# A decoder layer on Trainium2: the output projection's second norm, the order of the change to the up-projection, and the samples by DMA

## Chip, cores, metric

The kernel runs on one core of one Trainium2 chip. The metric is device microseconds of one execution, as the median of several.

## The reference, cut to what matters

One layer of a decoder: 1024 prompt tokens and 32 sample tokens (8 sequences of 4), model width 1024, feed-forward width 2816, all in float32.

```
x = x + gate1 * RMSNorm(Mix(RMSNorm(x) * (1 + scale1) + shift1))
x = x + gate2 * RMSNorm(ConvFFN(RMSNorm(x) * (1 + scale2) + shift2))

Mix:     mix = concat(pool_mixer, gated_conv, silu(layer_norm(conv31))) @ w_out
ConvFFN: up = h @ w_up
         gate, val = split(causal_dwconv3(up, past_ffn))
         ff = (silu(gate) * val) @ w_down
```

What is computed does not change. The change is in the layer norm of the third group of Mix, in the output projection with the norms behind it, and in the up-projection.

## The kernel before, in words

**Numbers.** Each float32 operand is split into two parts, high and low (`*_hi` is a cast on ACT, the scalar engine; `*_lo` is a subtraction on DVE, the vector engine), and a product takes three passes on PE, the tensor engine: high by high, high by low, low by high.

**Order.** Instructions of PE, ACT, DVE and SP (the engine that issues most DMAs) run in the order in which the program emits them. From the output projection on, this order is written by hand: `at(t, f, ...)` notes a step under a planned time `t`, and `play` emits all steps sorted by it. The planned times serve to sort; an engine works through its list and waits where a value is missing.

**Layer norm.** The variance of 1056 tokens goes through POOL as 96 rows of 11 (`ln_rstd`, L438) and comes back as a row by three small DMAs (L444). `ln_bc` (L446) spreads a third of the row over 128 partitions by a PE product with ones, into a PSUM buffer of `psb`, and `ln_apply` (L452) multiplies. After these come the loads of `w_out` row blocks 0, 1, 5, 6, 7 (`w_load`, L785) on SP, the pool mixer's products (`proj`, L605), the silu on ACT, and the products `mm2` (L833) of tiles 0 to 2 with `w_out` row blocks 2, 3, 4, then 1, 0, then 5, 6, 7. There are two buffers of `psb`.

**Output projection.** Eight tiles of 128 tokens and one of 32 (tile 8, the samples); a tile's product is 8 row blocks. `chain` (L962) lays out what follows for a tile: `sq1`, `rs` (sum of squares, then the scale by a power on POOL, L865), `gt`, `res` (L882, first norm and residual), `sq2`, `rs`, `xn2` (L889, product with the second scale), `tr` (L897, eight PE transpositions), `mod` (L911 on ACT or L908 on DVE), `h2_hi`, `h2_lo` (the split). Tiles come in pairs: `t13` and `t24` (L943, L948) form differences of an even and an odd tile, and `t_hi`, `t_lo` split these.

**Up-projection.** For each of 22 column tiles (gate and value, 128 columns each) a seven-product scheme: products 1 to 7 (`prod`, L1209, twelve PE steps each) take sums and differences of weight blocks (`s_sum`, `s_hi`, `s_lo`) and of token tiles. Product 1, 6, 5 and 3 accumulate one after the other in the first bank of one PSUM tile, product 2 takes its second bank, products 7 and 4 take the tile `U["z"]`. `snap` "a", "b", "c" (L1223, ACT) keep the first bank in between, `c11`, `c22`, `c21` (DVE, L1233) and `c12` (ACT, L1239) form the four blocks. The convolution `tap0`, `taps2` (L1280), `silu`, `gated` and `fsum` follow.

**Samples.** `smp` (L1253) multiplies the 32 sample tokens with both weight tiles, into one PSUM tile; `smp_ev` copies that to SBUF on ACT, `smp_t` (L1262) turns and sums it on PE by a product with `sel`, and `smp_out` (L1266) copies the result to the convolution's input.

**At the change of stage.** Products 1 and 2 of column tiles 0 and 1 come first (from planned time `t8`); between the first two stands `tr` of tile 7. Then from `b = t8 + 4 * DP` products 6, 5, 7, 3, 4 of tile 0, with `tr` of tile 8 and the samples of tiles 0 and 1 among them:

```
sample(0, b + DP + 0.9, b + 3 * DP + 2 * DS)
sample(1, b + 2 * DP + DS + 0.9, b + 4 * DP + 2 * DS, b + 5 * DP + 2 * DS + 7.0)
seq = [(prod, 0, 6), (DS + 0.9,), (prod, 0, 5), (DS,), (prod, 0, 7), (prod, 0, 3), (prod, 0, 4)]
```

In the loop of the later tiles the order on PE is product 6, samples of the next tile, 7, 5, product 1 of the next tile, 3, product 2 of the next tile, 4.

Of the kernel before, what the change touches and what calls it, by code (L numbers as in the profile page):

```python
# [10 lines left out]
F32 = mybir.dt.float32  # L11
# [39 lines left out]
def body(ctx: ExitStack, tc: tile.TileContext, a, o):  # L51
# [17 lines left out]
    one1 = lnp.tile([P, P], F32, name="one1")  # L69
# [11 lines left out]
    dve.memset(one1, 1.0)  # L81
# [9 lines left out]
    gd = tc.dram_tile([9, 2048], F32, name="gd")  # L91

# [860 lines left out]
    def t_hi(i):  # L953
        act.copy(ycol(0, i), h2_of(i))

    def t_lo(i):
        sub_to(ycol(1, i), h2_of(i), ycol(0, i).bitcast(F32))
# [4 lines left out]
    def chain(i, e, tt):  # L962
# [6 lines left out]
        at(e + 5.5, xn2, i)  # L969
# [3 lines left out]
        at(tt + 1.1, mod, i, 1)  # L973
        at(tt + 2.5, h2_hi, i)
        if i % 2:
            at(tt + 2.5, t13, i)
            at(tt + 3.0, h2_lo, i)
            at(tt + 3.6, t24, i)
# [3 lines left out]
        else:  # L982
            at(tt + 3.5, h2_lo, i)

    def chain_s(e):
        for dt, f in ((0, sq1), (2.2, rs), (2.4, gt), (3.7, res), (4.9, sq2), (6.0, rs), (6.8, xn2)):
            at(e + dt, f, 8)
        for q in range(2):
            at(e + 11.74, tr, 8, q)
            at(e + 12.4 + 0.1 * q, mod, 8, q)  # L990
# [59 lines left out]
    for k in (2, 3, 4):  # L1050
        for i in range(3):
# [4 lines left out]
            if k == 3:  # L1056
                at(t, ln_bc, i)
# [38 lines left out]
    for n, i in enumerate(order):  # L1096
# [16 lines left out]
    fs = {p: tc.dram_tile([FT // 2, P, 512], F32, name=f"fs{p}") for p in range(1, 8)}  # L1113
    U = {}
# [16 lines left out]
    def open_b():  # L1131
# [77 lines left out]
    def prod(i, p):  # L1209
# [5 lines left out]
        for k in range(4):  # L1215
# [5 lines left out]
    def snap(i, n):  # L1221
        t = pools["p3" if n == "a" else "p3b"].tile([P, 512], F32, name=f"sn{n}", bufs=1)
# [33 lines left out]
    def smp_ev(i):  # L1256
        t = pools["p3"].tile([P, P], F32, name="smp", bufs=2)
        act.copy(t, U["s"][:, P * (i % 2):P * (i % 2) + P])
        U["smp", i] = t

    def smp_t(i):
        pe.matmul(U["s"][:, 256:320], lhsT=U["smp", i], rhs=U["sel"].rearrange("p a n -> p (a n)"), start=True, stop=True)  # L1262

    def smp_out(i, v):
        e = e_of(i, v)
        act.copy(ext_parts(e, 2)[2], U["s"][:, 256 + 32 * v:288 + 32 * v].rearrange("p (s t) -> p s t", t=ST))  # L1266
# [59 lines left out]
    DP, DS = 2.75, 1.6  # L1326
# [7 lines left out]
    at(t8 + 14.5, open_z)  # L1334
    at(t8 + 14.51, open_b)
# [445 lines left out]
```

## Time and profile before

| | us |
|---|---|
| median of 3 runs (lowest, highest) | 1061.47 (1061.19, 1062.1) |
| the profiled execution | 1063.64 |
| its span, first to last instruction | 1061.8 |
| mean granted TensorE clock | 0.992 |
| PE busy | 1030.5 (97%) |
| DVE busy | 825.0 (78%) |
| ACT busy | 466.6 (44%) |
| POOL busy | 38.2 (4%) |
| DMA queue 1, share of 16 engines | 39.0% |

One execution is profiled; stretches and single instructions are read from it, while the median comes from other runs. Busy time of PE overlaps between neighbouring steps, so the distance of two starts tells what a step costs, and waits are listed by the engine that waits and the instruction that ended them. A granted clock of 1.00 is 2.4 GHz, 0.50 is 1.2 GHz.

### The profile page before, as it was taken

What the parts mean: (1) busy time and instruction counts of PE and PEld (TensorE: products, weight loads), DVE (VectorE), ACT (ScalarE), POOL (GpSimd) and SP (SyncE); (2) the same over time, 40 slices, a digit from 0 to 9 for tenths busy, and PEclk for the clock granted to TensorE, in tenths of its full rate; (3) what the DMA queues carried; (4) which work ended last, traced back from release to release, by engine and by line L of the source; (5) the groups of instructions that cost most, each with busy time, mean ns of one, the idle gap of its engine ahead of it and who ended that gap; (6) DMA issues with size and microseconds to landing.
All of it is one profiled execution on the core that took longest, in us unless ns stands there. A gap on an engine that the chain in (4) does not pass through costs nothing. (4 is left out here: it accounts for less than half of the span.)

```text
span 1061.8 us, 15512 instructions
## 1 busy us (share of the span) xinstructions
PE 1030.5 (97%) x6094; PEld 864.8 (81%) x6094; DVE 825.0 (78%) x1142; ACT 466.6 (44%) x835; POOL 38.2 (4%) x56
## 2 busy tenths in 40 slices
PE   5999999999999989999999999999999999999997
PEld 4999989997687668888888888888888787778885
DVE  5688898978547788888788788778878764987584
ACT  6331111115747745445454444544545464335551
POOL 3000000001011100000000000000000000020100
PEclk9999999999999989999999999999999999999999
DMA  8776652211512413323314223322323694325272
GB/s 334 262 228 194 193 185 88 63 41 17 184 43 99 156 54 99 109 64 127 110 60 129 91 79 115 104 80 92 114 74 110 228 412 179 109 73 161 90 267 100
DMA packets 68050, 141.10 MB, mean 133 GB/s; under 512 B 17156, under 2 KB 28676, under 8 KB 64904
## 3 DMA queue, kind: packets, MB, share of 16 engines
q1 hardware_dynamic: 66632, 135.77, 39.0%
q10 hardware_dynamic: 1344, 4.33, 1.0%
q8 instruction: 48, 0.79, 0.3%
q14 instruction: 26, 0.21, 0.1%
HBM read 110.18 MB, written 29.90 MB: 132 GB/s over the span
## 5 line engine op out<-in xcount | busy, mean ns | idle before, releaser
L1280 DVE SCALAR_TENSOR_TENSOR facc<-fext,par,facc 128x1072 f32<-128x1072 f32 x88 | 117.2, 1332 | 14.2 <-ACT facc L1273 12.7
L535 DVE SCALAR_TENSOR_TENSOR yb<-cext,par,yb 128x1024 f32<-128x1024 f32 x90 | 111.9, 1278 | 0.8
L279 PE MATMUL psa<-hh,whi 128*128 128x352 f32 x372 | 82.0, 328 | 0.0
L279 PE MATMUL psa<-hh,wlo 128*128 128x352 f32 x372 | 80.2, 323 | 0.0
L1532 PE MATMUL psd<-whi 128*128 128x512 f32 x204 | 80.1, 393 | 0.0
L279 PE MATMUL psa<-hl,whi 128*128 128x352 f32 x372 | 80.1, 323 | 0.0
L1532 PE MATMUL psd<-whi,wlo 128*128 128x512 f32 x204 | 79.6, 390 | 0.1
L1532 PE MATMUL psd<-wlo,whi 128*128 128x512 f32 x204 | 79.5, 390 | 0.1
L1513 ACT CAST whi<-fa 128x512 fp32r<-128x512 f32 x73 | 45.3, 621 | 70.9 <-PE psb L1532 24.6
L927 DVE TENSOR_TENSOR wlo<-fa,whi 128x512 fp32r<-128x512 f32 x73 | 49.9, 684 | 31.0 <-ACT whi L1513 31.0
L1218 PE MATMUL psc<-hh,sh 128*128 128x512 f32 x176 | 69.7, 396 | 2.8 <-DVE fext L1233 2.8
L1218 PE MATMUL psb<-hh,sh 128*128 128x512 f32 x176 | 71.3, 405 | 0.0
L1218 PE MATMUL psc<-hl,sh 128*128 128x512 f32 x176 | 69.6, 396 | 0.9 <-DVE hl L927 0.9
L1218 PE MATMUL psc<-hh,sl 128*128 128x512 f32 x176 | 69.4, 395 | 0.0
L1218 PE MATMUL psb<-hh,sl 128*128 128x512 f32 x176 | 68.8, 391 | 0.0
L1218 PE MATMUL psc<-bh,whi 128*128 128x512 f32 x176 | 68.6, 390 | 0.0
L1218 PE MATMUL psc<-bh,wlo 128*128 128x512 f32 x176 | 68.5, 389 | 0.0
L1218 PE MATMUL psc<-bl,whi 128*128 128x512 f32 x176 | 68.5, 389 | 0.0
L1218 PE MATMUL psb<-hl,sh 128*128 128x512 f32 x176 | 68.5, 389 | 0.0
L279 PEld LDWEIGHTS psa<-hh,whi 128*128 128x128 f32 x372 | 62.8, 189 | 6.4 <-issue 4.1
L279 PEld LDWEIGHTS psa<-hh,wlo 128*128 128x128 f32 x372 | 63.8, 188 | 0.0
L279 PEld LDWEIGHTS psa<-hl,whi 128*128 128x128 f32 x372 | 63.1, 188 | 0.0
(270 smaller groups left out, 2318.0 us busy)
## 6 DMA issues: line engine op xcount, KB each, us to landing
fa<-fs SPq DMA_DIRECT2D x73, 256.0 KB, 3.8
adaw<-in_ada SPq DMA_DIRECT2D x16, 1024.0 KB, 7.5
raw<-in_w_up SPq DMA_DIRECT2D x22, 512.0 KB, 3.6
rawb<-in_w_up SPq DMA_DIRECT2D x22, 512.0 KB, 3.7
fs<-facc SPq DMA_DIRECT2D x44, 256.0 KB, 2.5
b<-in_w_down SPq DMA_DIRECT2D x18, 512.0 KB, 7.3
fs<-whi SPq DMA_DIRECT2D x33, 256.0 KB, 2.3
adaw<-in_adag SPq DMA_DIRECT2D x8, 1024.0 KB, 7.1
```

The costliest lines, as they stand in the source:

```text
L279: pe.matmul(ps[:, c, 0:CW], lhsT=wt[:, k, :], rhs=h[:, k, c * CW:(c + 1) * CW], start=(k == 0 and n == 0), stop=(k == KT - 1 and n == 2))
L535: dve.scalar_tensor_tensor(out=y[:, 0:NPR], in0=e[:, k:k + NPR], scalar=par[:, off + k:off + k + 1], in1=y[:, 0:NPR], op0=ALU.mult, op1=AL ...
L927: dve.tensor_tensor(out=out, in0=x, in1=y, op=ALU.subtract)
L1218: pe.matmul(out, lhsT=w[:, ks], rhs=h(k), start=(p in (1, 2, 7) and k == 0 and n == 0), stop=(k == 3 and n == 2), skip_group_check=True)
L1280: dve.scalar_tensor_tensor(out=acc[:, 0:1072], in0=e[:, k:k + 1072], scalar=par[:, wo + k:wo + k + 1], in1=acc[:, 0:1072], op0=ALU.mult, o ...
L1513: act.copy(hi[:, 0:512], R[n, "raw"])
L1532: pe.matmul(ps, lhsT=s[:, cs], rhs=w, start=(first and m == 0), stop=(j == HK - 1 and m == 2), skip_group_check=True)
```

## The change

- The layer norm's row goes to DRAM by one DMA and comes back to all 128 partitions by a second, in place of three DMAs and the three products of `ln_bc`.
- `xn2` is sorted ahead of `h2_lo` of the tile before (planned 4.95 instead of 5.5 after the chain's start, `h2_lo` half a microsecond later); `t24` becomes `t2` and `t4`, and `t_hi`, `t_lo` can take half a tile.
- At the change of stage the order on PE becomes products 6, 7, three quarters of 5, `tr` of tile 8 (into the samples' PSUM tile), the rest of 5, both sample groups, 3, 4. Three lists give the order on DVE and ACT around it. Some temporary tiles move to buffers that are free then.
- `smp_ev` becomes a DVE transposition (in blocks of 32 by 32), a DMA to DRAM, and `smp_ld` brings four loads that gather the turned block; `smp_out` adds two pieces on DVE. `smp_t` and `sel` go, in all 22 column tiles.
- Planned times of later weight loads, casts and sums move for column tiles 0 to 2.

```diff
-        for c in range(3):
-            sync.dma_start(rows[32 * c:32 * c + 1, :], rt[32 * c:32 * c + 32, :])
-
-    def ln_bc(c):
-        rw = slice(32 * c, 32 * c + 1)
-        ln["r", c] = psb()
-        pe.matmul(ln["r", c][:, 0:CW], lhsT=one1[rw, :], rhs=rows[rw, :], start=True, stop=True,
-                  tile_position=(32 * c, 0))
+        sync.dma_start(rsd.rearrange("o (q n) -> (o q) n", n=11), rt)
+        ln["r"] = zc_tile()[:, 0:T]
+        sync.dma_start(ln["r"], rsd.broadcast_to([P, T]))
...
-        pt = psb()
-        pv = pt.rearrange("p (k n) -> p k n", n=P)[:, :, 0:rows]
+        if i < 8:
+            pv = psb().rearrange("p (k n) -> p k n", n=P)
+        else:
+            pv = U["s"][:, 256 + P * q:256 + P * q + P].rearrange("p (k n) -> p k n", n=rows)
...
-    def t24(i):
+    def t2(i):
         r0, r1 = h2_of(i - 1), h2_of(i)
-        sub_to(r1[:, 4:8], r1[:, 4:8], r0[:, 0:4])
-        sub_to(r0[:, 4:8], r0[:, 4:8], r1[:, 4:8])
+        st[i, "t2"] = r1[:, 4:8] if i < 7 else st[i, "t"][:, 0:512].rearrange("p (k n) -> p k n", n=P)
+        sub_to(st[i, "t2"], r1[:, 4:8], r0[:, 0:4])
+
+    def t4(i):
+        r0 = h2_of(i - 1)
+        sub_to(r0[:, 4:8], r0[:, 4:8], st[i, "t2"])
...
-        at(e + 5.5, xn2, i)
+        at(e + 4.95, xn2, i)
...
-            at(tt + 3.0, h2_lo, i)
-            at(tt + 3.6, t24, i)
+            at(tt + 3.55, h2_lo, i)
+            at(tt + 3.6, t2, i)
+            at(tt + 3.6, t4, i)
...
-            at(tt + 3.5, h2_lo, i)
+            at(tt + 4.0, h2_lo, i)
...
-        for dt, f in ((0, sq1), (2.2, rs), (2.4, gt), (3.7, res), (4.9, sq2), (6.0, rs), (6.8, xn2)):
+        for dt, f in ((0, sq1), (2.2, rs)):
...
         t = pools["p3"].tile([P, P], F32, name="smp", bufs=2)
-        act.copy(t, U["s"][:, P * (i % 2):P * (i % 2) + P])
-        U["smp", i] = t
-
-    def smp_t(i):
-        pe.matmul(U["s"][:, 256:320], lhsT=U["smp", i], rhs=U["sel"].rearrange("p a n -> p (a n)"), start=True, stop=True)
+        dve.transpose(out=t, in_=U["s"][:, P * (i % 2):P * (i % 2) + P])
+        sync.dma_start(smpd[i], t)
+
+    def smp_ld(i):
+        u = U["smp", i] = pools["p3"].tile([P, P], F32, name="smq", bufs=2)
+        for j in range(4):
+            sync.dma_start(u[32 * j:32 * j + 32].rearrange("m (q t) -> m q t", t=32),
+                           smpd[i].rearrange("(q m) (j t) -> j m q t", q=4, j=4)[j])
...
-        act.copy(ext_parts(e, 2)[2], U["s"][:, 256 + 32 * v:288 + 32 * v].rearrange("p (s t) -> p s t", t=ST))
+        dve.tensor_tensor(out=ext_parts(e, 2)[2], in0=u[:, 2 * v], in1=u[:, 2 * v + 1], op=ALU.add)
...
+    FIRST = [(s_sum, 0, 5), (t2, 7), (s_sum, 0, 6), (t_hi, 7, HI), (s_hi, 0, 6), (t_lo, 7, HI), (snap, 0, "a"), (s_lo, 0, 6),
+             (c11, 0), (s_sum, 0, 7), (t_hi, 7, LO), (s_hi, 0, 7), (t_lo, 7, LO), (s_lo, 0, 7), (gt, 8), (res, 8), (t_hi, 6, LO),
+             (s_hi, 0, 5), (snap, 1, "a"), (t_lo, 6, LO), (s_lo, 0, 5)]
+    SECOND = [(h2_hi, 7), (sq2, 8), (rs, 8), (xn2, 8), (t4, 7), (t_hi, 6, HI), (s_sum, 0, 3)]
+    THIRD = [(s_hi, 0, 4), (s_hi, 0, 3), (snap, 0, "c"), (h2_lo, 7), (s_lo, 0, 3), (t_lo, 6, HI), (open_b,), (c22, 0), (s_lo, 0, 4), (smp_ev, 0), (c11, 1)]
-    DP, DS = 2.75, 1.6
+    DP, DS, WD = 2.75, 1.2, 3.0
...
-        at(t8 - 3.9 + 2.2 * i, a_lo, i)
+        at(t8 - 3.9 + 5.0 * i, a_lo, i)
...
+    for n, (f, *args) in enumerate(FIRST):
+        at(b - 0.5 + 0.01 * n, f, *args)
+    for n, (f, *args) in enumerate(SECOND):
+        at(b + DP + 0.2 + 0.01 * n, f, *args)
+    at(b + 2.75 * DP, tr, 8, 0)
...
+    for n, (f, *args) in enumerate(THIRD):
+        at(b + 3 * DP + DS + 0.01 + 0.01 * n, f, *args)
...
-        at(t1 - 0.01, smp_t, i)
+        at(t + DS + 4.0, smp_ld, i)
...
+            sample(0, b + 3 * DP, b + 5 * DP + 2 * DS - 0.6, b + 5 * DP + 2 * DS + 0.1)
+            sample(1, b + 3 * DP + DS, b + 5 * DP + 2 * DS + 3.0, b + 5 * DP + 2 * DS + 7.0)
+            seq = [(prod, 0, 6), (prod, 0, 7), (prod, 0, 5, 0, 3), (2 * DS,), (prod, 0, 3), (prod, 0, 4)]
+            at(b + 2.8 * DP, prod, 0, 5, 3, 4)
...
-            weights(i + 1, b + 2 * DP + (DS if i else 2 * DS + 1.0))
+            weights(i + 1, b + 2 * DP + DS + WD * (i == 1) if i else b + 3 * DP + 2 * DS + 0.3)
```

## Rows read from the trace of the kernel before

**Rows 1.** PE's waits in the whole span: total us, times, longest

```profile
PE psc L1218 <- DVE fext L1233: 2.8, 1, 2.8
PE psb L897 <- DVE ms L864: 2.5, 2, 1.2
PE psb L607 <- DVE yb L454: 2.2, 1, 2.2
PE psb L897 <- DVE pt L889: 1.1, 1, 1.1
```

**Rows 2.** Table by stretch: length, busy PE, PEld, DVE, ACT, POOL, clock, DMA share, GB/s

```profile
371.48:408.34 36.86, 32.63 (x193) 25.26 (x192) 28.00 (x44) 18.50 (x37) 2.31 (x5) 0.91 0.21 68
431.36:451.90 20.54, 20.54 (x121) 16.96 (x119) 17.34 (x25) 9.88 (x19) 0.00 (x0) 1.00 0.34 116
```

**Rows 3.** PE in order of time: start, us, line, out<-in

```profile
262.60 0.85 PE L449 MATMUL psb<-row,one 1*128 1x352 f32 x2
...
282.35 0.61 PE L833 MATMUL psc<-rh,hh 128*128 128x512 f32 x2
```

**Rows 4.** ACT in order of time, around the layer norm's end

```profile
269.77 1.04 ACT L792 CAST rh<-w 128x1024 fp32r<-128x1024 f32 x1 [0.26 <-DMA w<-in_w_out]
...
273.45 1.28 ACT L458 ACT_TABLE_LOAD   x1
...
279.47 0.50 ACT L692 CAST hh<-yb 128x384 fp32r<-128x384 f32 x1
...
285.83 1.05 ACT L792 CAST rh<-raw 128x1024 fp32r<-128x1024 f32 x1 [2.16 <-DMA raw<-in_w_out]
```

**Rows 5.** SP's issues in order of time, then DMA issues with us to landing

```profile
256.37 1.91 SPq L444 DMA_DIRECT2D row<-rt  x3
...
259.06 1.16 SPq L785 DMA_DIRECT2D w<-in_w_out  x2
...
x1d<-px ACTq DMA_DIRECT2D x8, 512.0 KB, 2.6
...
row<-rt SPq DMA_DIRECT2D x3, 1.4 KB, 1.7
```

**Rows 6.** POOL, then DVE in order of time, second norm of tile 3

```profile
331.94 0.55 POOL L865 TENSOR_TENSOR rs<-ms,nhalf 128x1 f32<-128x1 f32 x1 [4.65 <-DVE ms L864]
...
332.58 1.22 DVE L927 TENSOR_TENSOR bl<-px,bh 128x1024 fp32r<-128x1024 f32 x1 [0.79 <-ACT bh L931]
333.72 0.74 DVE L889 TENSOR_SCALAR pt<-px,rs 128x1024 f32<-128x1024 f32 x1
```

**Rows 7.** DVE in order of time, second norm of tile 6

```profile
359.60 1.42 DVE L927 TENSOR_TENSOR px<-px 128x512 f32<-128x512 f32 x2
360.93 0.75 DVE L889 TENSOR_SCALAR pt<-px,rs 128x1024 f32<-128x1024 f32 x1
```

**Rows 8.** PE in order of time, product 6 of tile 1 and two sample groups

```profile
408.34 0.39 PE L1218 MATMUL psc<-hh,sh 128*128 128x512 f32 x1
...
410.83 0.39 PE L1218 MATMUL psc<-hh,sl 128*128 128x512 f32 x1
411.15 0.30 PE L1253 MATMUL psb<-raw,hs 128*32 128x128 f32 x2
...
431.36 0.33 PE L1262 MATMUL psb<-sel,smp 128*128 128x64 f32 x2
431.62 0.30 PE L1253 MATMUL psb<-raw,hs 128*32 128x128 f32 x2
...
432.63 0.50 PE L1218 MATMUL psb<-hh,sh 128*128 128x512 f32 x1
```

**Rows 9.** DVE, then ACT in order of time at the change of stage

```profile
372.80 0.75 DVE L889 TENSOR_SCALAR pt<-px,rs 128x1024 f32<-128x1024 f32 x1
...
378.03 0.59 ACT L1223 COPY sna<-psc 128x512 f32<-128x512 f32 x1 [2.18 <-PE psc L1218]
```

**Rows 10.** DVE in order of time, modulation of the samples

```profile
393.29 0.29 DVE L917 TENSOR_TENSOR hs<-psb,aT 128x128 f32<-128x128 f32 x1 [2.03 <-PE psb L897]
```

More of the change, by code (lines that the diff above doesn't have):

```diff
@@ L946, in t13, with t_src, t_hi, t_lo @@
         sub_to(r1[:, 0:4], r1[:, 4:8], r1[:, 0:4])
-    def t24(i):
+    def t2(i):
         r0, r1 = h2_of(i - 1), h2_of(i)
-        sub_to(r1[:, 4:8], r1[:, 4:8], r0[:, 0:4])
-        sub_to(r0[:, 4:8], r0[:, 4:8], r1[:, 4:8])
[L953 to L957, printed above, removed]
+        st[i, "t2"] = r1[:, 4:8] if i < 7 else st[i, "t"][:, 0:512].rearrange("p (k n) -> p k n", n=P)
[3 more added lines that the diff above has]
+        sub_to(r0[:, 4:8], r0[:, 4:8], st[i, "t2"])
+    def t_src(i, r):
+        return h2_of(i)[:, r] if i < 7 or r.start == 0 else st[i, "t2"]
+    def t_hi(i, r=slice(0, KT)):
+        act.copy(ycol(0, i)[:, r], t_src(i, r))
+    def t_lo(i, r=slice(0, KT)):
+        sub_to(ycol(1, i)[:, r], t_src(i, r), ycol(0, i)[:, r].bitcast(F32))
     def gate_s():
@@ L973, in chain @@
         at(tt + 1.1, mod, i, 1)
+        if i == 7:
+            at(tt + 2.5, t13, i)
+            return tt
         at(tt + 2.5, h2_hi, i)
@@ L1172, in s_sum @@
             dve.tensor_tensor(out=t, in0=a21, in1=a22, op=ALU.add)
+        elif p == 7 and i == 0:
+            t = U["s", i][7] = stream.tile([P, 1024], F32R, name="whi").bitcast(F32)[:, 0:512]
+            sub_to(t, a11, a21)
         elif p == 7:
@@ L1176, in s_sum @@
             sub_to(U["s", i][6], U["s", i][5], a11)
+        elif p == 3 and i == 0:
+            t = U["s", i][3] = stream.tile([P, 1024], F32R, name="whi").bitcast(F32)[:, 0:512]
+            sub_to(t, a12, U["s", i][6])
         elif p == 3:
@@ L1214, in prod @@
         out = four(ps)
-        for k in range(4):
+        for k in range(k0, k1):
             ks = slice(P * k, P * k + P)
@@ L1221, in snap @@
     def snap(i, n):
-        t = pools["p3" if n == "a" else "p3b"].tile([P, 512], F32, name=f"sn{n}", bufs=1)
+        if n == "c" and i == 0:
+            t = stream.tile([P, 1024], F32R, name="wlo").bitcast(F32)[:, 0:512]
+        else:
+            t = pools["p3b" if n == "c" else "p3"].tile([P, 512], F32, name=f"sn{n}", bufs=1)
         act.copy(t, x_of(i)[:, 0])
@@ L1338, in body @@
         at(t8 - 5.0 + 2.2 * i, a_hi, i)
-        at(t8 - 3.9 + 2.2 * i, a_lo, i)
+        at(t8 - 3.9 + 5.0 * i, a_lo, i)
         at(t1, prod, i, 1)
         at(t1 + DP, prod, i, 2)
-        at(t1 + DP + 0.1, snap, i, "a")
-        at(t8 + (6.1 if i == 0 else 14.6), c11, i)
+    for n, (f, *args) in enumerate(FIRST):
[3 more added lines that the diff above has]
+    at(b + 2.75 * DP, tr, 8, 0)
+    at(b + 2.75 * DP, tr, 8, 1)
+    at(b + 2.75 * DP, mod, 8, 0)
+    at(b + 2.75 * DP, mod, 8, 1)
+    for n, (f, *args) in enumerate(THIRD):
+        at(b + 3 * DP + DS + 0.01 + 0.01 * n, f, *args)
     def weights(i, t):
@@ L1356, in sample @@
         at(t, smp, i)
-        at(t + DS, smp_ev, i)
-        at(t1 - 0.01, smp_t, i)
+        if i:
+            at(t + DS + 0.05, smp_ev, i)
+        at(t + DS + 4.0, smp_ld, i)
         at(t1 + 0.6, smp_out, i, 0)
@@ L1363, in body @@
         if i == 0:
-            for p, ts, th, tl in ((5, 5.0, 6.1, 9.2), (6, 5.1, 6.0, 6.9), (7, 15.6, 15.7, 16.3), (3, 15.8, 16.8, 17.5), (4, 0, 12.0, 14.7)):
-                if p != 4:
-                    at(t8 + ts, s_sum, 0, p)
-                at(t8 + th, s_hi, 0, p)
-                at(t8 + tl, s_lo, 0, p)
-            sample(0, b + DP + 0.9, b + 3 * DP + 2 * DS)
-            sample(1, b + 2 * DP + DS + 0.9, b + 4 * DP + 2 * DS, b + 5 * DP + 2 * DS + 7.0)
-            seq = [(prod, 0, 6), (DS + 0.9,), (prod, 0, 5), (DS,), (prod, 0, 7), (prod, 0, 3), (prod, 0, 4)]
+            sample(0, b + 3 * DP, b + 5 * DP + 2 * DS - 0.6, b + 5 * DP + 2 * DS + 0.1)
+            sample(1, b + 3 * DP + DS, b + 5 * DP + 2 * DS + 3.0, b + 5 * DP + 2 * DS + 7.0)
+            seq = [(prod, 0, 6), (prod, 0, 7), (prod, 0, 5, 0, 3), (2 * DS,), (prod, 0, 3), (prod, 0, 4)]
+            at(b + 2.8 * DP, prod, 0, 5, 3, 4)
         elif i == FT - 2:
@@ L1396, in body @@
             elif p == 6:
-                at(done + (0 if j else 0.8), snap, j, "b")
-            elif p == 5:
+                at(done, snap, j, "b")
+            elif p == 5 and j:
                 at(done, snap, j, "c")
-                if j:
-                    at(done + 0.8, c22, j)
-            elif p == 7 and j == 0:
                 at(done + 0.8, c22, j)
```

35 lines of the change are left out of this document (14 added, 21 removed).

## Prediction

> **What bounds the kernel now.** First the whole: TensorE (PE) is busy 97% of the span (table of the profile), so time can be won only where PE waits, runs at its lower clock, or does work that the change takes away. PE's list of waits says where it waits [rows 1]: one wait of 2.2 us on a multiply of the layer norm (L454), three of 1.2, 1.2 and 1.1 us ahead of a tile's transposition (L897), one of 2.8 us at the up-projection's products (L1218). All lie between 260 and 390 us, where the change is. The table by stretch [rows 2] gives the last place its size: from the first product of the up-projection (371.48) to product 6 of column tile 1 (408.34) 36.86 us pass at a mean granted clock of 0.91, so some products ran at 1.2 instead of 2.4 GHz after the waits. In the loop behind it PE is busy for all of 20.54 us and DVE for 17.34: PE is the bound there, and only less PE work helps.
>
> **Part 1, the norm row.** Three broadcast products on PE go: the first starts at 262.60 and runs 0.85 us [rows 3], 2.4 us for three. The 2.2 us wait goes with them, since it was for a PSUM buffer that held a broadcast row. What is late next is ACT: the third pool-mixer product needs the PSUM buffer of the first, and ACT empties that only behind its cast of w_out row block 1, which begins at 269.77 [rows 4] as soon as that load has landed. The change makes these loads later. Before, SP issues three row DMAs from 256.37 and the w_out loads at 259.06 [rows 5]. After, one DMA to DRAM (0.6), a wait for its landing (1.7 for such a small one), the broadcast's issue (0.5) and out_n_p (0.7, the gap between the two rows) stand ahead of them: 256.37 + 0.6 + 1.2 + 0.5 + 0.7 = 259.4 if the landing counts from the issue's start, 259.9 if from its end. The broadcast also puts 540 KB ahead of them in the DMA engines: a 512 KB write lands in 2.6 us, 0.9 more than a tiny one [rows 5]. Together 0.4 to 1.8 us later; I take 1.5, and 3 as the bad end. ACT then runs cast (to 272.3), pool evacuation (0.55), and the row of work that took from the table load at 273.45 to the end of y0_hi(0) at 279.97, 6.5 us without a gap [rows 4]: y0_hi(0) ends at 279.45 instead. PE's first product with it stood at 282.35 [rows 3] and can now start at 279.65, 2.7 us earlier; at PE's half clock after its new wait (270.0 to 273.1) the three products before it still fit. The last w_out block's cast at 285.83 [rows 4] comes only some 0.5 us earlier, so half a microsecond is given back. **-2.2 us**, between +0.5 (loads over 3 us late) and -3.2.
>
> **Part 2, xn2 ahead of the former tile's subtraction.** For tile 3 the scale is ready at 332.5 (POOL 331.94 + 0.55), but DVE first does the 1.22 us subtraction from 332.58, and xn2 starts at 333.72 [rows 6]. In the new order it starts at 332.5, 1.2 us earlier, which is PE's whole wait; tile 5 repeats the pattern. For tile 6 two subtractions (1.42) lie between the scale's sum and xn2 at 360.93 [rows 7], and h2_lo holds the sum itself up: xn2 comes 1.2 to 1.8 us earlier against a wait of 1.1. The work put behind delays nobody: in front of the next tile's product DVE waits for PE. **-3.6 us** (1.2 + 1.2 + 1.1 and 0.1 at tile 1), bounds -2.4 and -3.7.
>
> **Part 3, the change to the up-projection.** At full clock a product takes 12 x 0.226 = 2.73 us (408.34 to 410.83 for eleven steps), a sample group 1.01 [rows 8]. PE's own work in the 36.86 us is nine products (24.6), two sample groups (2.0), two transpositions (0.8 and 0.7): 28.1. The rest, 8.8, is the wait of 2.8 and the ones after it, half clock, and two smp_t. Why PE waited: snap a(0) sits ahead of the modulation of tile 7 on ACT and waits until 378.03 for product 2, though it copies product 1's bank [rows 9]; so t13, t24, both t_hi and c11 come late, and product 6 waits for c11, which reads the same PSUM tile. In the new order ACT modulates tile 7 right after its transposition. I count DVE on from xn2(7), which ended at 373.5 [rows 9] and now ends near 372.3: a_lo(1) 1.2, sample sum 1.2, modulation 1.4 (from 374.55), first half of t13, a wait for ACT to 377.4, then seven subtractions and sums of 0.6 to 0.65 and c11: 381.95. PE, 1.1 earlier by part 2, has its four products and tile 7's transposition done at 382.15. The wait is gone with 0.2 us to spare. From there DVE is never idle: product 7's operands are ready at 383.9 (needed 384.9), product 5's at 387.5 (needed 387.6), xn2(8) at 389.5 (needed 389.65). The sample groups then wait for four modulations of tile 8 (0.29 each [rows 10], done 391.8 against 391.0): 0.95 us. 28.1 + 0.95 = 29.05 instead of 36.86, -7.8; as three steps have under 0.3 us to spare I take **-7.0**, bounds -4 (DVE 3 us late once) and -7.8.
>
> **Part 4, smp_t.** Its 22 pairs leave PE. From the pair to the next sample group pass 0.26 us; without one the change from product to sample group takes 411.15 - 410.83 - 0.23 = 0.09 [rows 8]. 20 x 0.17 = **-3.4 us** (two are in part 3). DVE gets a 128x128 transposition and two small adds per column tile. No row shows a DVE transposition; the nearest are the 128x128 operation from PSUM, 0.29, and a 1024-wide one, 1.22 [rows 10, 6]; I take 0.3, as the operand is the former's. The adds stand between 0.17 and 0.29 each. So 17.34 becomes about 18 of 20.3 us: still hidden; bound +1.8 for all three, hidden too. ACT loses 0.6.
>
> **Part 5, the new waits.** SP waits for the sample's landing before it issues the four loads; behind it stand later weight loads, which have 10 us. smp_out waits for the loads on DVE. In the loop they have some 16 us. For column tile 0 it is short: transposition to 395.1, write landed by 397.3, four issues and half a megabyte of weights ahead, data near 402.5. Behind smp_out on DVE stands c21(0), and for c21(0) waits product 7 of tile 1 at 403.2: **+0.5 us**, bounds 0 and +3.
>
> **Sum.** -2.2 - 3.6 - 7.0 - 3.4 + 0.5 = -15.7. The profiled execution took 1063.64 (span 1061.8), the median is 2.2 lower: 1047.9 for such an execution, 1045.8 for the median. All bad ends together: +0.5 - 2.4 - 4.0 - 3.0 + 3.0 = -5.9, 1055.6; all good ends: -3.2 - 3.7 - 7.8 - 3.8 = -18.5, 1043.0.
>
> **Rivals.** (a) DVE gets late in the transition: it has about 19 us of work in the 19 us from xn2(7) to the modulation of tile 8, and each microsecond there, or in the first samples' round trip, is PE's. With 4 us lost: 1049.8. For it: the small margins; against: all durations are measured. A row for the round trip's 128-byte pieces does not exist. The Trainium skill, "DMA: Bandwidth & Descriptors", section "Why small descriptors are slow (HBM only)", gives short pieces a fixed cost per packet, which would make this rival likelier; no run here shows it yet. (b) The w_out loads land 5 us late, as DMA was busy but slow there: part 1 turns from -2.2 to +1.5: 1049.5. (c) The change doesn't do what it says: xn2 moved ahead waits for POOL or ACT all the same, and PE's three waits stay: 1049.4. For tile 6 that can be, for 3 and 5 the gap ahead of the subtraction speaks against. (d) **Slower**: DVE becomes the bound of the loop. 17.34 us plus the new three operations must stay under 20.3; above 3.0 us each further microsecond costs 20 us over the loop. It eats the 15.7 us from 3.8 us on; at 4.1 the kernel takes 1067.8. The place would be smp_ev and smp_out ahead of c21 and c11. Rows speak against: it needs more than three 1024-wide operations. The Trainium skill speaks for it: "VectorE: DVE Perf Modes", section "Rules for kernel authors", sends 128x128 transpositions to TensorE if PSUM will do as their target, as it was before; by that rule part 4 would have been left out and the sum would be -12.3, and the table by stretch, with PE full and DVE not, is against it here.
>
> **How the numbers follow.** Forecast 0.60; (a) 0.17, (b) 0.09, (c) 0.08, (d) 0.04; 0.02 for several losses that meet near no change. 0.2% (2.1 us) is about what a measurement of this kernel can tell from no change. Faster 0.94, same 0.02, slower 0.04. The range goes from 1042, a little below all good ends, to 1052, which takes in (a), (b) and (c) and one more loss of 2 us: that leaves out (d) and the worst sums.
>
> **What would show it.** Right: no PE wait at L897 nor at the products up to tile 1, granted clock 1.00 in that stretch and about 29 us from the first product to product 6 of tile 1; a loop of 20.3 us; the w_out cast near 270 and a PE wait of some 3 us at the third pool-mixer product. Wrong: waits of PE on DVE at L1218 or at the sample group over 2 us, PE waits in the loop, or casts of w_out after 273.

## The result and the profile after

The changed kernel takes 1047.38 us (median of 6 executions, 1046.09 to 1051.2) against 1061.78 (6 executions, 1060.07 to 1062.86): 0.9874 of the time before, 95% interval 0.9853 to 0.9894. In a second set beside new runs of the kernel before it was 0.9884 (0.9866 to 0.9901). The prediction was 1045.8 with a range of 1042 to 1052. The profiled execution after took 1046.6 (span 1044.8, mean clock 0.996), the one before 1063.64.

First PE's list of waits after the change (engine, line, what waited, for whom; us in total, times, longest), without the ones that both kernels share:

```profile
PE psb L893 <- DVE pt L883: 2.0, 3, 0.9
PE psc L827 <- ACT hh L686: 1.5, 1, 1.5
...
PE psb L1225 <- DVE fext L1243: 0.6, 1, 0.6
PE psc L1225 <- DVE ms L858: 0.6, 1, 0.6
PE psc L1225 <- DVE fext L1243: 0.4, 1, 0.4
...
PE psb L1263 <- DVE hs L913: 0.2, 1, 0.2
```

Against [rows 1] the waits at the first pool-mixer product behind the layer norm (2.2) and at the up-projection (2.8) are gone. The three ahead of the transpositions are not: 3.6 us became 2.0. One of 1.5 us on ACT's cast `hh` is new. The next view is the table by stretch: the change to the up-projection (first product to product 6 of tile 1), the 20 us behind it, and one column tile of the loop (busy us of PE, weight loads, DVE, ACT, POOL, then granted clock, DMA share, GB/s):

```profile
364.48:394.27 29.79, 29.01 (x189) 23.25 (x188) 26.75 (x47) 15.71 (x30) 2.17 (x5) 1.00 0.21 67
399.00:419.00 20.00, 19.50 (x84) 15.25 (x83) 19.64 (x29) 11.11 (x19) 0.00 (x0) 1.00 0.31 86
439.36:459.63 20.27, 20.27 (x117) 16.50 (x117) 16.47 (x26) 9.91 (x17) 0.00 (x0) 1.00 0.29 85
```

Against [rows 2] the first stretch went from 36.86 us at a clock of 0.91 to 29.79 at 1.00. In the loop PE is busy for the whole of the 20.27 us and DVE for 16.47. That is a column tile with one `fsum`, while [rows 2] shows one with three; like beside like, DVE went from 16.25 to 16.47 and, in the next tile, from 17.27 to 17.48. Between the two lies a stretch with DVE full (19.64 of 20): that is new.

To see where each part of the gain lies, I cut every profile at four instructions that all kernels have: the first product of the output projection, the first product of the up-projection, the sample group of column tile 3 and that of column tile 21. A is the time from the first to the second, B from the second to the third. The third piece is 368.28 us in every kernel with smp_t and 364.92 in every one without.

| kernel | time to before (95%) | A us | B us |
|---|---|---|---|
| before | 1 | 115.18 | 60.14 |
| after | 0.9874 (0.9853 to 0.9894) | 108.67 | 54.60 |
| e1 norm row alone | 0.9989 (0.9979 to 0.9998) | 111.49 | 60.13 |
| e2 product ahead alone | 0.9981 (0.9970 to 0.9992) | 111.04 | 60.00 |
| e3 samples by DMA alone | 0.9953 (0.9938 to 0.9968) | 112.95 | 58.68 |
| e4 all but the new order | 0.9927 (0.9913 to 0.9942) | 108.80 | 59.64 |
| e5 after again | 0.9884 (0.9866 to 0.9901) | 108.15 | 54.59 |
| e6 loads first | 0.9852 (0.9836 to 0.9869) | 105.95 | 54.50 |
| e7 even tiles in the old order | 0.9858 (0.9844 to 0.9873) | 106.57 | 54.21 |
| e8 c21 ahead | 0.9861 (0.9847 to 0.9875) | 107.55 | 54.42 |
| e9 short pieces last | 0.9855 (0.9829 to 0.9882) | 106.09 | 54.40 |
| e10 all mends | 0.9830 (0.9804 to 0.9857) | 104.29 | 54.06 |
| e11 mends, weights first | 0.9835 (0.9821 to 0.9849) | 104.32 | 54.22 |
| e12 before, short pieces last | 0.9977 (0.9964 to 0.9989) | 111.94 | 60.30 |

A and B come from one profiled execution each, the ratio from 4 to 12. A is itself uncertain: before and e3 have the same code there and differ by 2.23 (below), and so have after, e5 and e8, which differ by 1.12.

### The profile page after: what moved, and what is told of

Read it like the earlier page. It is cut to its first block, busy times and chain, and to the rows that moved or that the text cites. A ratio compares the mean times of both kernels' runs of the same rounds, so it can differ in the third digit from the quotient of the medians.

```text
span 1044.8 us, 15559 instructions
## 1 busy us (share of the span) xinstructions
PE 1019.3 (98%) x6044; PEld 853.3 (82%) x6044; DVE 828.9 (79%) x1208; ACT 458.4 (44%) x771; POOL 37.2 (4%) x56
## 5 line engine op out<-in xcount | busy, mean ns | idle before, releaser
L1287 ACT ACTIVATE facc<-fext,par 128x1072 f32<-128x1072 f32 x44 | 52.6, 1195 | 26.0 <-DVE fext L1243 22.6
```

The costliest lines, as they stand in the source:

```text
L1287: act.activation(acc[:, 0:1072], e[:, 2:1074], AF.Copy, scale=par[:, wo + 2:wo + 3])
```

## The experiments

**e1: the norm row alone**, in the kernel before.

```diff
-        for c in range(3):
-            sync.dma_start(rows[32 * c:32 * c + 1, :], rt[32 * c:32 * c + 32, :])
+        sync.dma_start(rsd.rearrange("o (q n) -> (o q) n", n=11), rt)
+        ln["r"] = zc_tile()[:, 0:T]
+        sync.dma_start(ln["r"], rsd.broadcast_to([P, T]))
...
-                at(t, ln_bc, i)
```

> The kernel before with the norm row's round trip through DRAM alone. Theory (read from the two traces): the loads of w_out are not late behind the new transfer, their casts on ACT begin near 266.6 and 268.6 instead of 268.46 and 269.77, PE's wait of 2.2 us at the third pool-mixer product and the half clock after it are gone, and the first product of the up-projection comes 4.0 to 5.0 us earlier: 0.9953 to 0.9962 of the time before. Rival (the prediction's term): the casts come 1 to 1.5 us later than before, PE waits some 3 us at that product, and 2.2 us are won: 0.9979. If the gain in the pair of traces was a matter of the execution, the casts lie near 268.5 again.

Measured: 0.9989 (0.9979 to 0.9998), -1.2 us: neither the 4.0 to 5.0 us read from the pair of traces nor, in the middle, the 2.2 of the prediction, which is the interval's end. In ACT's timeline, first of the kernel before, then of e1, and in PE's of e1 (start, us, engine, line, what; in brackets the idle time before and its releaser):

```profile
268.46 1.05 ACT L792 CAST rh<-w 128x1024 fp32r<-128x1024 f32 x1 [5.33 <-DMA w<-in_w_out]
```

```profile
267.28 1.05 ACT L786 CAST rh<-w 128x1024 fp32r<-128x1024 f32 x1 [4.15 <-DMA w<-in_w_out]
269.93 1.05 ACT L786 CAST rh<-w 128x1024 fp32r<-128x1024 f32 x1 [1.60 <-DMA w<-in_w_out]
...
271.48 0.86 PE L601 MATMUL psb<-w,pw 128*128 128x352 f32 x2 [0.79 <-ACT yb L602]
```

Both kernels start the output projection at 256.3, so the first cast comes 1.2 us earlier than before, the second no earlier than in [rows 4], and the third pool-mixer product waits 0.8 us for ACT's evacuation behind it. That is the chain the prediction described, with less delay in it. Some 2 us of what the pair of traces showed belong to the execution of the kernel before that was profiled; for the remainder no run shows a place. The table by stretch, first for the kernel before, then for e3, whose code is the same there:

```profile
272.00:277.00 5.00, 5.00 (x14) 3.63 (x15) 2.23 (x2) 4.09 (x6) 0.00 (x0) 0.66 0.00 1
```

```profile
272.00:277.00 5.00, 5.00 (x21) 3.77 (x21) 1.98 (x2) 4.34 (x6) 0.00 (x0) 1.00 0.00 0
```

Before, PE ran 14 matmuls in these 5 us at a mean granted clock of 0.66, so for some two thirds of the stretch at the lower level, 1.2 GHz; in e3 it ran 21 at 1.00. The wait ahead of them was 2.22 us in the one [rows 1] and 1.85 in the other (1.81 in e2, also with the clock at 1.00). From the end of the wait to the first product with `rh` 5.98 us passed before (271.99 to 277.97) and 4.37 in e3 (271.74 to 276.11): the lower clock cost 1.6.

**e2: the product ahead alone**, in the kernel before.

```diff
-        at(e + 5.5, xn2, i)
+        at(e + 4.95, xn2, i)
...
-            at(tt + 3.0, h2_lo, i)
+            at(tt + 3.55, h2_lo, i)
...
-            at(tt + 3.5, h2_lo, i)
+            at(tt + 4.0, h2_lo, i)
```

> The kernel before with the second norm's product ahead of the former tile's subtraction alone (tiles 1 to 7). Theory: the gap between successive tiles' transpositions falls from 10.44 to 9.8 us for tiles 3 and 5, from 9.02 to 8.7 for tile 6, and stays for tiles 2 and 4; three PE waits of 0.5 to 0.9 us remain, since DVE now idles 0.73 us for POOL's scale on the even tiles and passes that on; -1.9 us in all: 0.9982. Rival (the prediction's term): the three waits are gone, the gaps of tiles 3 and 5 fall to 9.2, and 3.6 us are won: 0.9966.

Measured: 0.9981 (0.9970 to 0.9992), -2.0 us. The theory's 0.9982 is at its middle; the prediction's 0.9966 lies outside. PE's timeline at the transpositions of tiles 3, 5 and 6:

```profile
332.27 1.06 PE L897 MATMUL psb<-ident,pt 128*128 128x128 f32 x8 [0.55 <-DVE pt L889]
...
349.76 1.06 PE L897 MATMUL psb<-ident,pt 128*128 128x128 f32 x8 [0.53 <-DVE pt L889]
...
358.33 1.06 PE L897 MATMUL psb<-ident,pt 128*128 128x128 f32 x8 [0.67 <-DVE pt L889]
```

**e3: the samples by DMA alone**, in the kernel before: smp_ev, smp_ld and smp_out of the change, without smp_t and sel.

> The kernel before with the samples' way through DRAM alone, in the old order at the change to the up-projection. Theory: the loop's period falls from 20.46 to 20.27 us in 18 periods, -3.4, and two more smp_t go ahead of it, -0.4; in the old order smp_out of column tile 0 has its data before DVE comes to it, as the sample group lies earlier than in the new order, so no wait appears: 0.9964. Rival: the wait of smp_out(0) on the loads and DVE's fuller stretch behind it belong to the samples' way in whatever order, and cost 1.5 us here too: 0.9978.

Measured: 0.9953 (0.9938 to 0.9968), -5.0 us; the theory's 0.9964 is inside, the rival's 0.9978 is not. The third piece shrank by 3.36, and B by 1.46 instead of growing (some 0.8 of it is a shorter spell at the lower clock in product 6, which lies ahead of the samples; in e4 B shrank by 0.5): no wait of PE behind smp_out appears in its list. So the samples' way costs nothing that shows in the old order, and the 1.5 us that the stretch behind product 6 of tile 1 lost in the changed kernel come from the two together. The profiles give 4.0 of the 5.0 us a place: 3.36 in the third piece and the rest of B.

**e4: all but the new order.** The edits of e1, e2 and e3 together.

> The three parts together in the kernel before: norm row, product ahead, samples by DMA, with the old order at the change to the up-projection. If the parts add up, -4.6 - 1.9 - 3.8 = -10.3: 0.9903, and the new order is worth the rest, 3 to 4 us, although the stretch from the first product to product 6 of tile 1 was 7.1 us shorter (36.86 to 29.79), for 1.5 are given back behind it and some of what the stretch lost before is lost elsewhere now. Rival: the new order is worth its full 7 us, and these three parts together win only 6.5: 0.9938. That stretch takes 36 to 37 us here by both.

Measured: 0.9927 (0.9913 to 0.9942), -7.7 us: the theory's 0.9903 lies outside and the rival's 0.9938 inside, though the new order is not worth the rival's full 7 us either. The sum of the three alone is 1.2 + 2.0 + 5.0 = 8.2, so the parts add up as far as this can be told. What the new order is worth is the rest to the changed kernel: 4.6 to 5.6 us by the two ratios of that, 5.04 by B. The stretch from the first product to product 6 of tile 1 takes 36.48 us here (39.29 to the sample group of tile 2, less 2.81 for product 6) and 29.79 after: 6.7 won, of which 1.7 are given back behind it.

**e5: the changed kernel again.** No edit.

> The changed kernel itself, once more, as the base of the three that follow. Its profile shows how far one execution differs from another: by one theory the two w_out casts start 10.8 and 12.8 us behind the first product of the output projection here too; by the other they move with the loads, as in the run with the norm row alone (11.0 and 13.6), and some of what the first pair of traces gave to the norm row (4.6 us) is the old kernel's execution, whose products 269 to 277 ran at the lower clock.

ACT's timeline there:

```profile
267.80 1.05 ACT L786 CAST rh<-w 128x1024 fp32r<-128x1024 f32 x1 [3.67 <-DMA w<-in_w_out]
269.60 1.05 ACT L786 CAST rh<-w 128x1024 fp32r<-128x1024 f32 x1 [0.76 <-DMA w<-in_w_out]
```

That is 10.5 and 12.3 us behind the first product (257.3). Over after, e1, e4, e5 and e8 the second cast lies between 12.07 and 13.64: the second load does move, by up to 1.6 us between executions of the same code up to there, and the first by 0.6.

**e6: the loads first.** The store of out_n_p behind the first two w_out loads; with it the broadcast of the norm row went behind them too.

```diff
-        sync.dma_start(o["n_p"][p], ext_new(u, PP))
+        if p:
+            sync.dma_start(o["n_p"][p], ext_new(u, PP))
...
     at(0.0, w_load, 1)
+    at(0.0, lambda: sync.dma_start(o["n_p"][0], ext_new(pus[0], PP)))
```

> The changed kernel with the store of out_n_p (60-byte pieces, 67.5 KB) issued behind the first two w_out loads instead of ahead of them. Theory: the short pieces are what keeps the queues at 90 to 200 GB/s between 262 and 268; without them ahead the casts start 2 us earlier or more, near 8.5 and 10.5 us behind the first product, the PE wait of 1.5 us on y0_hi(0) is gone, and the kernel is 1.5 us faster than after (0.9860). Rival: the broadcast's 528 KB and the loads' own size set the landing; the casts stay within 0.5 us, and so does the time.

Measured: 0.9852 (0.9836 to 0.9869), 2.7 us below e5 by the medians (1044.99 and 1047.7), 2.2 by A; the wait of PE on y0_hi(0) is gone. SP's and ACT's timelines:

```profile
256.15 0.85 SPq L780 DMA_DIRECT2D w<-in_w_out  x2
...
262.40 2.00 ACT L787 CAST rh<-w 128x1024 fp32r<-128x1024 f32 x2
```

The casts start 6.7 and 7.7 us behind the first product (255.66), earlier than the 8.5 and 10.5 expected, and wait for no load. As two transfers had moved, the cause was still open; e9 takes them apart.

**e9: the short pieces last.** As e6, with the broadcast kept ahead of the loads.

> The run with the store of out_n_p behind the loads also had the broadcast of the norm row issued behind them: SP took the two loads in while it waited for the row's landing, at 256.15 instead of 258.35. Here the broadcast stays ahead of the loads, and out_n_p alone goes behind them. Theory (short pieces): the loads follow the broadcast by 0.4 us instead of 1.0 and meet no 60-byte pieces; 1.5 MB at 400 GB/s are in by 262.5, the casts start near 6.5 and 8 us behind the first product, no PE wait on y0_hi(0), and the time is that of the run with both moved (0.9852). Rival (the broadcast): its 528 KB and the wait for the row are what makes the loads late; the casts start at 9.5 to 12.5 as in the changed kernel, and the time stays near 0.988.

SP's and ACT's timelines:

```profile
258.35 0.33 SPq L446 DMA_DIRECT2D zc<-rsd  x1
258.78 0.86 SPq L782 DMA_DIRECT2D w<-in_w_out  x2
259.73 0.55 SPq L1038 DMA_DIRECT2D out_n_p<-pu  x1
...
264.27 1.06 ACT L789 CAST rh<-w 128x1024 fp32r<-128x1024 f32 x1 [0.57 <-DMA w<-in_w_out]
266.67 1.05 ACT L789 CAST rh<-w 128x1024 fp32r<-128x1024 f32 x1 [1.34 <-DMA w<-in_w_out]
```

The casts start 7.4 and 9.8 us behind the first product (256.88), 3.1 and 2.5 earlier than in e5, though the 528 KB of the broadcast are still ahead. SP issues the loads 0.6 and 0.9 us earlier than in e5, so 2.5 and 1.6 us of this are the 67.5 KB of out_n_p, in 1152 pieces of 60 bytes. The broadcast holds the loads up as well: they take 5.5 and 7.4 us from issue to landing here and 4.6 on average in e6, where it is behind them, and the second cast lies inside the rival's range. The time shows nothing of that: A is 106.09 and the ratio 0.9855 (0.9829 to 0.9882), as in e6, since in both PE no longer waits for y0_hi(0). So the short pieces are what cost the kernel time, as the theory has it. (The Trainium skill, "DMA: Bandwidth & Descriptors", section "Why small descriptors are slow (HBM only)", gives each packet a fixed overhead; this run agrees, with 1.6 and 2.5 us for these pieces, about what the broadcast costs with eight times the bytes.)

**e12: the same store moved in the kernel before.** The edit of e6, norm row on PE as before.

> The kernel before with the store of out_n_p behind the first two w_out loads, and nothing else: the norm row stays on PE. Theory: in the old kernel, too, the 2.2 us wait of PE at the third pool-mixer product comes from the late loads (cast of the first at 268.5, its remainder on DVE until 270.7, and behind that on DVE the multiply that frees the broadcast row's buffer), not from the broadcast products as such; with the loads early the wait and the half clock after it are gone, the time from the first product of the output projection to that of the up-projection falls from 113.0 to 115.2 to 110.5 or less, and the kernel is 2.5 us faster or more (0.9976 or below), more than the norm row through DRAM alone gave (0.9989). Rival: the wait belongs to the broadcast rows in PSUM; it stays at 1.5 us or more, and the time changes by less than 1 us.

First PE's timeline in the kernel before at the wait, then ACT's and PE's in e12:

```profile
271.99 0.86 PE L607 MATMUL psb<-w,pw 128*128 128x352 f32 x2 [2.22 <-DVE yb L454]
```

```profile
265.34 1.05 ACT L793 CAST rh<-w 128x1024 fp32r<-128x1024 f32 x1 [0.96 <-DMA w<-in_w_out]
...
269.90 0.75 PE L608 MATMUL psb<-w,pw 128*128 128x352 f32 x2
...
273.86 0.75 PE L608 MATMUL psb<-w,pw 128*128 128x352 f32 x2
```

The wait of 2.2 us stood at the first of the three pool-mixer products, not at the third, as the expectations of e1 and e12 have it. Here neither of the two (269.90, 273.86) waits, with the broadcast rows still in PSUM: 0.9977 (0.9964 to 0.9989), -2.4 us, about the 2.5 expected. That is twice the middle of what the norm row gave alone, though the two intervals (-3.8 to -1.2 and -2.2 to -0.2) overlap. A, 111.94, is over the 110.5 expected; 0.3 us of that lie at tile 6, and the rest was not followed.

**e7: even tiles in the old order.** h2_lo of tiles 1 and 3 ahead of the product of tiles 2 and 4.

```diff
-            at(tt + 3.55, h2_lo, i)
+            at(tt + (2.9 if i < 5 else 3.55), h2_lo, i)
```

> The changed kernel with h2_lo of tiles 1 and 3 put back ahead of the next even tile's product; for tiles 3, 5, 6 and 7 the product stays ahead. Theory: on even tiles the product ahead makes DVE idle 0.73 us for POOL's scale, and the next odd tile's first product with the gate inherits it; with the old order there, the two PE waits of 0.55 us ahead of the transpositions of tiles 3 and 5 are gone (gaps 9.77 to 9.2), -1.1 us in all. Rival: these waits come from the odd tile's own chain (squares, sum, POOL, product); then the gaps stay at 9.7 and even tiles get later by 0.1.

```profile
329.67 1.06 PE L893 MATMUL psb<-ident,pt 128*128 128x128 f32 x8
...
346.66 1.06 PE L893 MATMUL psb<-ident,pt 128*128 128x128 f32 x8
...
354.97 1.06 PE L893 MATMUL psb<-ident,pt 128*128 128x128 f32 x8 [0.38 <-DVE pt L883]
```

The two waits of tiles 3 and 5 are gone, and the gaps ahead of them fell from 9.77 and 9.76 to 9.27 and 9.22: the theory holds. A fell by 1.6 to 106.57, 0.5 of it at tile 6. The time, 0.9858 (0.9844 to 0.9873), is 1.6 us below e5 by the medians, but the intervals overlap.

**e8: c21 ahead.**

```diff
-                at(done, c21, j)
+                at(done - (0.2 if j == 0 else 0), c21, j)
```

> The changed kernel with c21 of column tile 0 put ahead of smp_out of column tile 0 on DVE. Theory: the wait of 2.22 us for the sample's loads no longer holds c21, so PE's 0.6 us wait at product 7 of tile 1 is gone; DVE does c21 in the idle time, and the backlog behind it (0.4 us wait at product 3 of tile 2) shrinks as well: -0.6 to -1.1 us, the time from the first product to the fourth sample group 54.6 to 53.7. Rival: the 1.5 us that the first samples cost come from DVE being full from 399 to 419; then the wait only moves to a later product, and the stretch stays at 54.4 or more.

PE's and ACT's timelines:

```profile
397.27 1.19 ACT L1287 ACTIVATE facc<-fext,par 128x1072 f32<-128x1072 f32 x1 [3.11 <-DVE fext L1280]
...
400.50 0.56 ACT L1233 COPY snb<-psc 128x512 f32<-128x512 f32 x1
...
401.12 0.50 PE L1225 MATMUL psc<-hh,sh 128*128 128x512 f32 x1 [0.55 <-ACT snb L1233]
```

The theory fell: the wait of 0.6 us at product 7 is gone, and 0.55 comes back one product later, since ACT's tap0 waits 3.1 us for the same samples and the copy of product 6 is queued behind it. B is 54.42 instead of 54.59. The median is 1.4 us below e5 all the same; 0.6 of that lie in A, where the code is that of e5, and some such difference between executions has to be allowed for where e6 and e7 are held against e5 by their times.

**e10: all mends**: e6, e7, e8 and four edits more. The core of those:

```diff
+        if i == 4:
+            ld_a(0, act)
+            ld_a(1, act)
...
-    at(t8 - 12.0, ld_a, 0)
-    at(t8 - 11.9, ld_a, 1)
...
+        if (i, p) == (0, 1):
+            steps.sort(key=lambda s: s[1])
...
-        at(t + DS + 4.0, smp_ld, i)
+        at(t + DS + (4.0 if i else 1.55), smp_ld, i)
...
-            tw = b + 12.6 + 1.1 * (i == 1) if i else b + 17.3
+            tw = b + 12.6 + 1.1 * (i == 1) if i else b + 19.1
```

> The changed kernel with all that the runs before found, and three edits more: loads of w_out ahead of the broadcast and of out_n_p; old order on tiles 2 and 4; c21(0) ahead of smp_out(0); first two w_up loads issued from ACT behind the write of tile 4's residual instead of ahead of tile 5's; product 1 of column tile 0 takes its four steps pass by pass, so that the passes with wlo come last; the loads of sample 0 ahead of the next weights, and the cast of the third w_up block behind the copy of product 6. Theory: -2.4 (loads), -1.1 (tiles 3 and 5), -0.9 (tile 6: the write of tile 5's residual lands in 3 us instead of 6, and the modulation does not wait), -0.5 (product 1), -0.6 to -1.2 (first samples): 5.5 to 6.1 below the changed kernel, 0.9825 of the kernel before. Rivals: the write of tile 5 takes 6 us whatever is ahead of it, and the gap of tile 6 stays at 8.3 or more; each mend only uncovers the next wait, and the sum is under 4 us (0.985 or above).

Measured: 0.9830 (0.9804 to 0.9857); the median of 1043.34 is 4.4 us below e5. The interval holds the theory's 0.9825 and also the rival's 0.985. Tile 5's modulation follows its transposition at once now, and tile 6's wait is gone (its gap is 7.74 us, 8.76 after). The write of tile 5's residual lands in 3.8 us instead of 6.2, so the loads ahead of it had held it up. PE's wait in product 1 is gone too. First ACT's timeline at that modulation, then PE's waits:

```profile
344.73 2.90 ACT L911 ACTIVATE px<-psb,bT,aT 128x128 f32<-128x128 f32 x8 [0.53 <-PE psb L897]
```

```profile
PE psb L1270 <- DMA raw<-in_w_up: 1.7, 1, 1.7
...
PE psb L897 <- DVE pt L887: 0.2, 1, 0.2
```

The edit to the samples' loads won nothing: with them ahead, the weights of tile 2 come late, and PE waits 1.7 us for those.

**e11: the weights first again.** As e10, without the change to smp_ld.

> As the run with all the mends, but with the samples' loads behind the weights of column tile 2 again, as the changed kernel has them. Theory: there the weights came behind the samples' write and four loads, and PE waited 1.7 us for them at the sample group of tile 2, more than the samples gained; now that wait is gone, the samples come 1.5 us later and hold nobody up, since c21(0) is ahead of them on DVE and the copy of product 6 ahead of the cast on ACT: from the first product to the fourth sample group 52.5 us instead of 54.06, and 0.9815 of the kernel before. Rival: the late samples bring the 0.4 to 0.6 us waits at products of tiles 1 and 2 back, and the stretch stays above 53.2.

```profile
402.85 0.50 PE L1232 MATMUL psc<-bh,wlo 128*128 128x512 f32 x1 [1.65 <-DVE wlo L927]
...
398.58 2.70 DVE L1301 SCALAR_TENSOR_TENSOR facc<-fext,par,facc 128x1072 f32<-128x1072 f32 x2
...
401.61 1.19 DVE L927 TENSOR_TENSOR wlo<-raw,whi 128x1024 fp32r<-128x1024 f32 x1
```

The theory fell here too, and the rival's number is the one measured: B is 54.22. The wait of 1.7 for the weights is gone, and one of 1.65 took its place: I had put the cast of the third w_up block later on ACT, so its remainder came behind both pairs of taps on DVE. e10 without either edit was not tried. The theory's 0.9815 lies outside the interval (0.9821 to 0.9849). Both are 4 to 6 us faster than the changed kernel by the ratios (0.9830 and 0.9835 against 0.9874 and 0.9884), and so the best that ran.

## Why the prediction was right, and where it was not

The time was right within 2 us, and of the five parts two were right by size; three were 1.0 to 1.6 us too good. Of the signs named, the clock of 1.00 in the stretch, its length of about 29 us (29.79) and the loop of 20.3 us came. PE's waits at the transpositions (2.0 us) and in product 1 (0.56) were not to be there, and the wait of some 3 us at the third pool-mixer product did not come.

**Norm row: -2.2 forecast, -1.2 measured alone** (-2.2 to -0.2), and the lateness that it reckoned with did not come: the first load landed earlier, the second on average no later. "The change makes these loads later. [...] Together 0.4 to 1.8 us later; I take 1.5" failed. Behind the first product of the output projection the first cast starts at 11.74 to 12.16 us with three row DMAs and at 10.46 to 11.05 with the broadcast, 1.2 earlier; the second at 12.95 to 13.47 and 12.07 to 13.64. ACT's chain behind it held. From the profile after:

```profile
266.61 1.05 ACT L786 CAST rh<-w 128x1024 fp32r<-128x1024 f32 x1 [3.96 <-DMA w<-in_w_out]
268.61 1.06 ACT L786 CAST rh<-w 128x1024 fp32r<-128x1024 f32 x1 [0.96 <-DMA w<-in_w_out]
...
270.13 1.28 ACT L452 ACT_TABLE_LOAD   x1
...
276.06 0.50 ACT L686 CAST hh<-yb 128x384 fp32r<-128x384 f32 x1
...
276.61 0.73 PE L827 MATMUL psc<-rh,hh 128*128 128x512 f32 x2 [1.50 <-ACT hh L686]
```

From the table load to the end of y0_hi(0) pass 6.4 us (6.5 forecast), and PE waits for that cast. Taken from the profiled execution before, A fell by 3.7 us in e1; of that, 1.6 are the half clock that this execution had and e2 and e3 had not, and 0.4 its longer wait. The prediction noted that its execution was 2.2 us over the median, but gave the surplus to no place. "The 2.2 us wait goes with them, since it was for a PSUM buffer that held a broadcast row" is half the reason: e12 keeps the rows in PSUM and has no wait. The buffer was held by the multiply, the multiply stood behind w_lo on DVE, and w_lo behind the late load. Part of the sign is in SP's queue: the row's DMA takes 0.33 us there and not the 0.6 assumed, and it has landed 1.4 us after the start of its issue, so the loads are issued 2.54 us behind the first product of the output projection instead of 2.76, earlier and not 0.3 to 0.8 later. The 0.9 us put down to the broadcast were not too much: e9 against e6 gives 1.3 and 2.4 between issue and landing, though e6 has another order of issue. That the first cast gains a whole microsecond more would follow if the short pieces now meet the broadcast instead of the loads; this is only argued, no run shows it by itself (moving the store brought the first cast forward by 5 us without the broadcast, in e12 against e3, and by 3.1 with it, in e9 against e5).

**Product ahead: -3.6 forecast, -2.0 measured alone** (-3.2 to -0.8). The step that failed is "The work put behind delays nobody: in front of the next tile's product DVE waits for PE". DVE's and PE's timelines after, from tile 4 to tile 5:

```profile
334.76 0.75 DVE L883 TENSOR_SCALAR pt<-px,rs 128x1024 f32<-128x1024 f32 x1 [0.73 <-POOL rs L859]
335.43 0.68 DVE L923 TENSOR_TENSOR bl<-px,bh 128x512 fp32r<-128x512 f32 x1
336.15 1.42 DVE L923 TENSOR_TENSOR px<-px 128x512 f32<-128x512 f32 x2
337.96 1.22 DVE L923 TENSOR_TENSOR hl<-px,hh 128x1024 fp32r<-128x1024 f32 x1 [0.40 <-ACT hh L957]
339.10 0.15 DVE L858 TENSOR_SCALAR ms<-ss 128x1 f32<-128x1 f32 x1
339.17 1.21 DVE L869 TENSOR_TENSOR pt<-psc,G 128x1024 f32<-128x1024 f32 x1
...
346.08 1.07 PE L893 MATMUL psb<-ident,pt 128*128 128x128 f32 x8 [0.55 <-DVE pt L883]
```

On an even tile the subtraction had filled the time in which DVE waits for POOL's scale. Now DVE idles those 0.73 us, everything behind is later, and the next odd tile's product with the gate (339.17) stands behind it on DVE; PE sees it at 346.08. True on odd tiles, the sentence was false on even ones: e7 takes the order back there, and both waits are gone. Rival (c) named POOL's scale, and so was half right (2.0 us of waits are left). For tile 6 ACT's modulation of tile 5 held up as well: it waits 2.9 us for the write of that tile's residual.

```profile
349.08 1.16 ACT L907 ACTIVATE px<-psb,bT,aT 128x128 f32<-128x128 f32 x3 [2.87 <-DMA x1d<-px]
```

That wait is old (2.66 us in the trace before, as the first two w_up loads are issued 3.1 us ahead of the write in both), and e10, which moves those loads away, ends it. The prediction asked what is late next for the norm row, but not for tile 6: with xn2's 1.1 us gone, the modulation of tile 5 was.

**Change to the up-projection: -7.0 forecast, -7.07 between the two profiles and -6.7 against e4.** The mechanism came as described: clock 1.00, PE's waits 0.56 (third pass of product 1, behind h2_lo(6) and a_lo(0) on DVE) and 0.23 at the sample group, against one of 0.95 forecast there. The three steps with under 0.3 us to spare held, and rival (a) did not come. The closeness of the number is in part luck: PE is busy for 29.0 us of the stretch, where 28.1 of its own work were counted, and the 0.8 us taken off for the small margins, which were not needed, made up for most of that.

**smp_t: -3.4 forecast as 20 times 0.17; 18 times 0.19 is what the loop gave** (20.46 to 20.27 us by period). DVE's transposition, for which no row stood, takes what was assumed (0.3):

```profile
389.90 0.31 DVE L1269 STREAM_TRANSPOSE smp<-psb 128x128 f32<-128x128 f32 x1
```

The rule of the Trainium skill that was weighed ("VectorE: DVE Perf Modes", section "Rules for kernel authors": 128x128 transpositions on TensorE) does not decide this case: PE is the bound here, and DVE turns blocks of 32 by 32, while the DMAs put these in place. 0.31 us on DVE in a loop where it is busy for 16.5 or 17.5 of 20.3 us cost nothing that shows, and rival (d) with it is out.

**First samples: +0.5 forecast, +1.5 measured**, inside its bounds of 0 and 3. The first term was right, the second was not seen. From the profile after:

```profile
397.71 0.29 DVE L1280 TENSOR_TENSOR fext<-smq 128x32 f32<-128x32 f32 x2 [2.22 <-DMA smq<-smpd]
...
398.75 0.47 PE L1225 MATMUL psb<-hh,sh 128*128 128x512 f32 x1 [0.59 <-DVE fext L1243]
...
416.15 0.47 PE L1225 MATMUL psc<-hh,sh 128*128 128x512 f32 x1 [0.41 <-DVE fext L1243]
```

DVE idles 2.2 us for the loads, c21 behind them costs PE 0.59: that is the 0.5. But DVE then has 19.64 us of work in 20 and cannot make the idle time up, and 17 us later PE waits 0.41 for it again. That this second wait stems from the idle time is argued from DVE's order and not shown; the remaining 0.5 lies in shorter stalls that were not followed. e8, e10 and e11 fit it: each takes one wait away, another of 0.5 to 1.7 us appears, and B stays within 54.06 to 54.60.

**The sum.** -15.7 forecast; -14.4 by the first medians, -12.8 by the second set. As the three parts that failed lie on one side, the forecast was low; its range held. Their 3.6 us would have made -12.1: that the first medians came within 2 us is in part the spread between executions. Why two of the six executions of the changed kernel took 1050.8 and 1051.2 us is open: neither was profiled.

## What to carry to other kernels

Before work is put behind a step that moves up, look at what the step waits for: if the work had filled that wait, the wait becomes idle time, and whoever is next on that engine inherits it. A store in small pieces belongs behind the loads that the next stage waits for: that move alone gave 2.4 us in the old kernel, where taking three products off the bound engine gave 1.2 (the intervals overlap). And a gain of microseconds read from one pair of profiles can be half an accident of the execution: profile the same code twice before a part of the change is credited with it.

## What the runs showed of the hardware

With 67.5 KB in 1152 pieces of 60 bytes issued ahead of them, two 512 KB loads took 2.5 and 1.6 us longer from issue to landing (e5 against e9). With 528 KB of broadcast ahead they took some 1.3 and 2.4 us longer (e9 against e6): an eighth of the bytes cost about as much. PE's granted clock fell to a mean of 0.66 over 5 us behind a wait of 2.22 us in one execution, which cost 1.6 us, and stayed at 1.00 behind waits of 1.81 and 1.85 us in the same place of two others; what made the difference is not shown. The scale's way over POOL, from the end of the sum on DVE to the start of the product there, takes 0.66 to 0.73 us for a single column.
